# A hybrid decoder layer on one core: means formed with the first job, weights ahead of the quarters, and two groups of loads reordered

## The chip, the cores and the metric

The kernel runs on one core of a Trainium2 chip. The metric is the device time of one execution in microseconds (us); the median of several executions is compared. The engines are TensorE (PE; its weight loads are listed as PEld), VectorE (DVE), ScalarE (ACT), GpSimd (POOL) and SyncE (SP), which issues nearly all DMA transfers from one queue, in order.

## The reference, cut to what matters

One decoder layer over 1,104 tokens (16 meta, 1,024 prompt, 64 sample tokens), width 1,024:

```python
x = x + 0.5 * rmsnorm(swiglu(rmsnorm(x, f1_pre), f1_wg, f1_wu, f1_wd), f1_post)
m, ... = mixer(rmsnorm(x, m_pre), w_in, ..., w_out, ...)   # attention heads + gated short conv
x = x + rmsnorm(m, m_post)
x = x + 0.5 * rmsnorm(swiglu(rmsnorm(x, f2_pre), f2_wg, f2_wu, f2_wd), f2_post)

def rmsnorm(x, g):            # the mean runs over the 1,024 features of a token
    return x * rsqrt(mean(x * x) + eps) * g
def swiglu(x, wg, wu, wd):    # wg, wu: 1024 x 2816, wd: 2816 x 1024
    return (silu(x @ wg) * (x @ wu)) @ wd
```

The mixer projects with `w_in` (24 blocks of 128 columns: q, k, v of four heads, and three conv inputs), runs differential attention over the prompt and over a paged cache for the sample tokens, and projects back with `w_out`. Weights and data are float32.

## The kernel before, in words

**Layout.** Features lie on the 128 partitions, eight chunks `c` of 128 features; tokens lie along the free dimension. The tokens are cut into two halves `p` of 552, each half into two groups `g` of 276. Tile `Y[p]` (`yv`) holds a half's activations, `X[p]` its prepared operands.

**Stages, in order:** gate and up projection 1 (`phase`), down projection 1 (`down`), input projection of the mixer (`phase`), attention, output projection (`down`), gate and up projection 2 (`phase`), down projection 2 (`down`). The places where one hands its result to a `phase` are called hand-overs below: the start of the kernel is the first, down 1 to the input projection the second, the output projection to gate and up 2 the third.

**A norm.** `heads` takes the eight chunks of a half one after the other: ACT squares each (line 221), DVE adds the squares into `ss2` (line 222), ACT multiplies the chunk by the norm's gain in place (line 266). The factor rsqrt(mean) is not applied there: `mean_r` forms it with a matmul against a tile of 1/1024 (line 204) and Ln, Exp and Square on ACT (lines 197 to 199), two DVE operations (200, 201), and stores it in `R[p]`; it is multiplied into the product of a projection, after the matmul. At hand-overs two and three a half's chunks first pass `ready`: the norm of the stage before (lines 543 and 546 on DVE, its own mean kept in `R[p]`), and a store of the chunk to DRAM.

**A job.** A job is a pair of column blocks `u` for a half `p`. Most are done by `seven`: the 2x2 block scheme with seven products instead of eight. A product is four contraction steps, each of three matmuls on high and low parts (`three`, lines 169 to 171). It needs `quarters(p)`: sums of blocks of `Y[p]`, split into high and low part by ACT (line 175) and DVE (line 176), four steps for a half, 7 ACT and 11 DVE operations each; and it needs seven weight pieces, formed likewise from the raw weights in `WR` into `W` (`weights_piece`, lines 326 to 332). While the quarters of the first half and these pieces are not there yet, the first jobs of a phase are `plain`: float32 matmuls (line 296) straight on the gained chunks of `Y`, two per phase, three in the first. `plain` traces a chunk's matmuls and then some steps of the background work (`heads`, then `quarters`). A job's results are read by `Hidden`, `Unit2` and others; for the seven products the first reading is line 420, into the temporaries `n1` (two buffers) and `n5`, which `quarters` uses too.

**Order.** Within an engine the instructions run in the order of a planner, which sorts the traced program by its own estimate of when each is ready, earlier traced work first; a few edges are fixed by hand (`in_turn` for the matmuls, `issue_after`, `keep_in_program_order`). Buffers of one tag are handed on in the order of the program. SP's queue is in order as well: a transfer that waits holds those behind it.

**Weights at a phase's start.** Unit 0 or 1 comes from a copy `early[...]` in DRAM, loaded into `late_raw` (the upper part of `W`); the other is loaded into `WR`.

**Attention and output projection.** `cst` (identity, masks) lies in `WR` from column 1470 on, so the two raw buffers of `load_item` in `down` (`WR` from 0 and from 1024, in turn) partly overlap it.

Of the kernel before, what the change touches and what calls it, by code (L numbers as in the profile page):

```python
# [43 lines left out]
def hybrid_step(ctx: ExitStack, tc: tile.TileContext, ins, outs, n_pool):  # L44
# [104 lines left out]

    last_pe, last_dma = [None], [None]  # L150

# [104 lines left out]

    def heads(p, ready, gain, parts=((0, 1),)):


        ss2 = temp("ss2", HT)  # L260
        for gs in parts:
            t = slice(gs[0] * G, gs[-1] * G + G)
            for n, c in enumerate(ready(gs)):
                x = lay["yv"][p][:, c, :]
                sq_add(ss2, x, n == 0, gs)
                act.activation(x[:, t], x[:, t], AF.Copy, scale=gains[:, gain, c:c + 1])
                yield
            yield
            mean_r(lay["R"][p], ss2, gs)
            yield  # L270

    class Background:
# [15 lines left out]
    def plain(u, p, raw, use, outer, step):  # L288
# [11 lines left out]
        if outer:  # L300
            banks.update({(n, g): bank("mm")[:, :G] for g in range(2) for n in range(2)})
            for n, c in enumerate(PAIR_K):
                in_turn(part, [c], range(2))
                if n:
                    step()
                    if n > 2:
                        step()
            for g in range(2):
                use.plain(g, banks[0, g], banks[1, g])
        else:  # L310
            for g in range(2):
                banks.update({(n, g): bank("mm")[:, :G] for n in range(2)})
                for i in range(0, 8, 2):
                    in_turn(part, PAIR_K[i:i + 2], [g])
                    step()
                use.plain(g, banks[0, g], banks[1, g])

    def weights_of(src):
        dma(wraw, src)

    def weights_piece(n):
# [24 lines left out]
    def phase(n, src, early, late, uses, background, loaded=False, tail=iter(())):  # L346
# [6 lines left out]
        if not loaded:  # L353
            weights_of(src(1 - late))
        dma(late_raw, early)
        for u, p in [(0, 0), (0, 1), (1, 0)][:2 + late]:
            background.need(("h", p))
            if p and not late:
                for m in range(5):
                    weights_piece(m)  # L360
            plain(u, p, raws[u], uses(u, p), p == 0 and u == 0, background.step)
        if late:
            seven([(2, 0), (2, 1), (1, 1)] + [(u, p) for u in range(3, n) for p in range(2)], src, uses, background,
                  tail=tail)
        else:
# [111 lines left out]

    def down(src, blocks, base, order, place, w_src, reuse, g_post, g_pre, res, dst):

# [10 lines left out]
        inputs = [(p, b, i) for p in range(2) for b in range(nb) for i in range(blocks[b])]  # L490
        wt, raws, put = {}, [], []

# [19 lines left out]
        def load_input():  # L512
            p, b, i = inputs.pop(0)
            slot = xs[p][:, base(b) + i]
            dma(f32(slot[:, 0, :]), src(b, i, p))
            put.append(slot)

# [38 lines left out]
        def begin():  # L556
# [5 lines left out]
            yield  # L562
            for n in range(max(blocks[0], 3)):
                if n < 3:
                    split_item()
                    load_item()
                if n < blocks[0]:
# [71 lines left out]
    for c in PAIR_K:  # L639
        dma(lay["yv"][1][:, c, :], ins["x1"][:, c, :])  # L640
    background = Background((("h", 0), heads(0, lambda gs: entering(0), G_F1PRE)),
                            (("h", 1), heads(1, lambda gs: entering(1), G_F1PRE)),
                            (("x", 0), quarters(0)), (("x", 1), quarters(1)))
# [207 lines left out]

    dma(cst, ins["consts"])

# [262 lines left out]
    for step, job in enumerate(jobs):  # L1116
        nxt = step // 9 + 1
        if nxt < H:
# [21 lines left out]
    def place(p, b, q):  # L1140
        if q == 0:
# [3 lines left out]
    begin, run = down(both, (4, 4), lambda b: 4 * b, lambda p, b: (1, 2, 3, 0) if p and not b else (0, 1, 2, 3), place,  # L1145
                      lambda b, q: ins["w_out"][b, q], True, G_MPOST, G_F2PRE, x_spill, x_mid)
    for _ in begin:
# [94 lines left out]
```

## Time and profile before

| | |
|---|---|
| median of 3 runs | 2297.01 us (2293.79 to 2299.85) |
| profiled execution | 2293.83 us, span 2292.1 us |
| PE busy | 2136.1 us, 93% of the span |
| DVE busy | 1404.7 us, 61% |
| ACT busy | 929.5 us, 41% |
| POOL busy | 299.8 us, 13% |
| mean granted TensorE clock | 0.960 |

The span is the profiled stretch from the first to the last instruction of one execution. Busy shares are means over all stages; the stages around the change have shares of their own. The granted clock is 1.00 at 2.4 GHz and 0.50 at 1.2 GHz.

### The profile page before, as it was taken

To read this page: it belongs to the slowest core of one execution; us is meant where nothing else is said; L and a number is where in the kernel's file an instruction comes from. 1 tells how busy PE (TensorE), PEld (TensorE's weight loads), DVE (VectorE), ACT (ScalarE), POOL (GpSimd) and SP (SyncE) were. 2 spreads that over 40 slices of the span, in tenths; PEclk is the share of its full clock that TensorE was granted. 3 is DMA by queue.
4 is the path that set the end of the run, shared out by engine and by line. 5 is a ranking of instruction groups with operands and counts; after the bars stand their busy time and mean duration, and the time that the engine had idled before them with its cause. 6 is when DMAs were issued, how large, how long until landed. Compare 5 with 4: busy or idle time off the path is not lost.

```text
span 2292.1 us, 41517 instructions
## 1 busy us (share of the span) xinstructions
PE 2136.1 (93%) x16126; PEld 2038.4 (89%) x16126; DVE 1404.7 (61%) x2973; ACT 929.5 (41%) x1960; POOL 299.8 (13%) x419
## 2 busy tenths in 40 slices
PE   6899999999999979999799978749999999999997
PEld 5799999999999959999667768739999999999997
DVE  5766556655567775466457656765665665645756
ACT  7433333334254442333235555553333333332522
POOL 0111111110000004443302110001111111100000
PEclk9899999999999989999789889879999999999998
DMA  7121222235444313321567332112122222543443
GB/s 276 55 81 67 81 81 68 81 116 197 130 144 142 131 51 120 124 86 60 191 206 274 125 137 102 67 35 78 67 81 81 68 80 81 175 144 127 141 148 98
DMA packets 115240, 263.48 MB, mean 115 GB/s; under 512 B 14514, under 2 KB 56114, under 8 KB 107602
## 3 DMA queue, kind: packets, MB, share of 16 engines
q1 hardware_dynamic: 109698, 244.92, 31.7%
q0 software_dynamic: 5344, 15.90, 1.9%
q8 instruction: 126, 2.06, 0.4%
q14 instruction: 72, 0.59, 0.1%
HBM read 206.47 MB, written 61.97 MB: 117 GB/s over the span
## 4 chain that ended last, share of the span: by engine, by line
PE 51%; issue 31%; DVE 7%; POOL 5%; DMA 3%; ACT 2%; SPq 1%; POOLq 0%; ACTq 0%; DVEq 0%
PE mm L169 13%; PE mm L170 13%; PE mm L171 13%; POOL u L440 3%; POOL n L440 3%; PE po L982 2%; PE mm L296 2%; PE qk L929 2%; DVE X L176 2%; PE fl L967 1%; PE sa L1059 1%; PE st L204 1%; PE sa L1024 1%; DVE Y L546 1%; DVE Y L543 1%
## 5 line engine op out<-in xcount | busy, mean ns | idle before, releaser
L169 PE MATMUL mm<-X,W 128*128 128x276 f32 x3868 | 1130.1, 292 | 27.8 <-ACT W L175 10.5
L170 PE MATMUL mm<-X,W 128*128 128x276 f32 x3868 | 1127.2, 291 | 2.8 <-DVE X L176 2.8
L171 PE MATMUL mm<-X,W 128*128 128x276 f32 x3868 | 1126.6, 291 | 1.9 <-DVE W L176 1.9
L169 PEld LDWEIGHTS mm<-X,W 128*128 128x128 f32 x3868 | 732.0, 189 | 31.0 <-ACT W L175 11.4
L170 PEld LDWEIGHTS mm<-X,W 128*128 128x128 f32 x3868 | 733.0, 190 | 4.3 <-DVE X L176 4.0
L171 PEld LDWEIGHTS mm<-X,W 128*128 128x128 f32 x3868 | 733.3, 190 | 3.2 <-DVE W L176 3.2
L176 DVE TENSOR_TENSOR W<-WR,W 128x512 fp32r<-128x512 f32 (+3 forms) x421 | 329.1, 793 | 116.4 <-ACT W L175 114.8
L175 ACT ACTIVATE W<-WR 128x512 fp32r<-128x512 f32 (+3 forms) x421 | 284.1, 689 | 249.6 <-PE mm L170 134.8
L420 ACT ACTIVATE n<-mm 128x276 f32<-128x276 f32 x210 | 84.2, 401 | 317.5 <-PE mm L171 299.0
L586 DVE TENSOR_TENSOR Y<-Y,mm 128x276 f32<-128x276 f32 x288 | 126.3, 439 | 128.1 <-PE mm L171 123.4
L440 POOL TENSOR_TENSOR u<-u,R 128x276 f32<-128x276 f32 x93 | 75.1, 807 | 493.2 <-ACT u L471 265.3
L440 POOL TENSOR_TENSOR n<-n,R 128x276 f32<-128x276 f32 x83 | 65.4, 787 | 547.2 <-ACT n L449 547.2
L170 PE MATMUL mm<-X 128*128 128x276 f32 x416 | 121.9, 293 | 2.7 <-DVE X L176 2.7
L169 PE MATMUL mm<-X 128*128 128x276 f32 x416 | 123.0, 296 | 1.5 <-ACT X L175 1.5
L423 DVE TENSOR_TENSOR n<-mm,n 128x276 f32<-128x276 f32 x105 | 46.8, 445 | 125.7 <-PE mm L171 113.9
L171 PE MATMUL mm<-X 128*128 128x276 f32 x416 | 121.4, 292 | 0.0
L221 ACT ACTIVATE sq<-Y 128x276 f32<-128x276 f32 x168 | 68.2, 428 | 86.4 <-DVE Y L586 58.7
L176 DVE TENSOR_TENSOR X<-X 128x552 fp32r<-128x552 f32 x104 | 75.5, 728 | 38.4 <-ACT X L175 37.9
L169 PE MATMUL mm<-X,X 128*128 128x276 f32 x320 | 93.9, 293 | 0.0
L170 PE MATMUL mm<-X,X 128*128 128x276 f32 x320 | 93.1, 291 | 0.0
L171 PE MATMUL mm<-X,X 128*128 128x276 f32 x320 | 93.1, 291 | 0.0
L929 PE MATMUL qk<-q,q 64*128 64x336 f32 (+10 forms) x360 | 69.9, 385 | 15.5 <-ACT q L175 11.1
(174 smaller groups left out, 2669.3 us busy)
## 6 DMA issues: line engine op xcount, KB each, us to landing
WR<-in_w_gu SPq DMA_DIRECT2D x43, 1024.0 KB, 4.8
WR<-in_w_dn SPq DMA_DIRECT2D x48, 640.0 KB, 3.9
X<-hid SPq DMA_DIRECT2D x88, 276.0 KB, 4.1
kp<-in_cache_k SPq DMA_DIRECT2D x64, 256.0 KB, 3.9
vp<-in_cache_v SPq DMA_DIRECT2D x64, 256.0 KB, 4.4
hid<-u SPq DMA_DIRECT2D x93, 138.0 KB, 1.8
hid<-n SPq DMA_DIRECT2D x83, 138.0 KB, 1.7
WR<-in_w_in SPq DMA_DIRECT2D x11, 1024.0 KB, 4.9
```

Of the source, the lines that this page charges most:

```text
L169: nc.tensor.matmul(ps, lh, rh, start=first, stop=False, **kw)
L170: nc.tensor.matmul(ps, lh, rl, start=False, stop=False, **kw)
L171: last_pe[0] = nc.tensor.matmul(ps, ll, rh, start=False, stop=last, **kw).ins
L175: tc.keep_in_program_order(act.activation(hi, raw, AF.Copy))
L176: on.tensor_tensor(lo, raw, f32(hi), op=ALU.subtract)
L221: act.activation(sq, src[:, s], AF.Square)
L296: last_pe[0] = nc.tensor.matmul(banks[n, g], w, lay["yv"][p][:, c, g * G:g * G + G], start=c == PAIR_K[0], stop=c == PAIR_K[-1]).ins
L420: act.activation(t, ps, AF.Copy)
L423: dve.tensor_tensor(self.n1, ps, self.n1, op=ALU.add)
L440: on.tensor_tensor(t, t, lay["R"][p][:, g * G:g * G + G], op=ALU.mult)
L586: dve.tensor_tensor(y, y, ps, op=ALU.add)
L929: last_pe[0] = nc.tensor.matmul(pw[m], a[r, q0:q0 + P], b[r, k0:k1], start=n == 0, stop=n == 2, tile_position=(m * DH, 0)).ins
```

## The change

1. The mean of `heads` is no longer traced at the end of its chunks. A new function `rms` traces it where the factor is first read: in `plain` behind the matmuls of a half's first job (for the second half, behind each group of it), and for the first half of a `down` stage behind tile 7 of the last block. The sums of squares wait in `ss2`, at the kernel's start in `R[p]` itself (`at_r`).
2. In `phase` the weight pieces 0 to 4 are traced ahead of the last plain job in every phase (in the first phase: unit 2 is loaded into `WR` there, and its pieces are no longer left to `seven`). `upto` limits how far the background steps go within each plain job: `heads` of the second half in the first, the first half's quarters in the second, and so on.
3. The load of the early weights into `late_raw` is issued behind the load of the others (`issue_after(last_load[0])`).
4. In the last block of `down`, second half, the steps of `ready` begin one tile later (n > 8), with two at the last tile.
5. Attention: `cst` is a tile of its own and is loaded behind q, k and v. The first piece of `w_out` is loaded at step 4 of the 36 attention steps and split at step 12; `down` is told so (`have`), takes it off its list and splits its four inputs first.

```diff
+    def rms(p, gs):
+        if p in sums_of:
+            mean_r(lay["R"][p], sums_of[p], gs)
+            if gs[-1]:
+                del sums_of[p]
...
-        ss2 = temp("ss2", HT)
+        ss2 = sums_of[p] = lay["R"][p] if at_r else temp("ss2", HT)
...
-            yield
-            mean_r(lay["R"][p], ss2, gs)
-            yield
...
+        def upto(self, name):
+            return lambda: self.step() if any(n == name for n, _ in self.named) else None
...
+            rms(p, (0, 1))
             for g in range(2):
                 use.plain(g, banks[0, g], banks[1, g])
...
+                rms(p, (g,))
                 use.plain(g, banks[0, g], banks[1, g])
...
-        dma(late_raw, early)
-        for u, p in [(0, 0), (0, 1), (1, 0)][:2 + late]:
+        with tc.issue_after(last_load[0]):
+            dma(late_raw, early)
+        jobs = [(0, 0), (0, 1), (1, 0)][:2 + late]
+        for u, p in jobs:
             background.need(("h", p))
-            if p and not late:
+            if (u, p) == jobs[-1]:
+                if late:
+                    weights_of(src(2))
                 for m in range(5):
                     weights_piece(m)
-            plain(u, p, raws[u], uses(u, p), p == 0 and u == 0, background.step)
+            last = ("x", 1) if (u, p) == jobs[-1] else ("x", 0) if p else ("h", 1)
+            plain(u, p, raws[u], uses(u, p), p == 0 and u == 0, background.upto(last))
...
-                        if n % 4 == 3 if nb > 2 else n % 2 if b else n < 10:
+                        if n % 4 == 3 if nb > 2 else n % 2 if b else n < 8:
                             first.step()
-                        if p and b == nb - 1 and g:
+                        if p and b == nb - 1 and n > 8:
                             second.step()
+                            if n == 15:
+                                second.step()
                         if p and b == nb - 1 and n == 7:
+                            rms(0, (0, 1))
                             second = Background(*junction(1))
...
+    cst, = ring("cst", 1, K_W)
...
-    cst = WR[:, 1470:]
...
-    dma(cst, ins["consts"])
...
     load_v(0)
+    dma(cst, ins["consts"])
...
+        if step == 4:
+            dma(WR[:, :1024], ins["w_out"][0, 0])
+        if step == 12:
+            w = W[:, 1024:2048], W[:, 0:1024]
+            halves(w[0], w[1], WR[:, :1024], dve)
+            first_w = {(0, 0, 0): (w[1], w[0])}
```

## Rows read from the trace of the kernel before

**Rows 1.** The page: span, PE's busy time, DVE's group of weight splits.

```profile
span 2292.1 us, 41517 instructions
...
PE 2136.1 (93%) x16126; PEld 2038.4 (89%) x16126; DVE 1404.7 (61%) x2973; ACT 929.5 (41%) x1960; POOL 299.8 (13%) x419
...
L176 DVE TENSOR_TENSOR W<-WR,W 128x512 fp32r<-128x512 f32 (+3 forms) x421 | 329.1, 793 | 116.4 <-ACT W L175 114.8
```

**Rows 2.** PE's waits, whole span: total us, times, longest us.

```profile
PE st L204 <- DVE ss L222: 77.0, 6, 24.0
PE qk L929 <- ACT q L175: 11.1, 1, 11.1
PE mm L169 <- ACT W L175: 10.5, 3, 7.7
```

**Rows 3.** Timeline, first hand-over: start us, duration us, instruction [idle before <-releaser].

```profile
17.90 1.28 ACT L191 ACT_TABLE_LOAD   x1
...
31.92 0.76 ACT L266 ACTIVATE Y<-Y,gains 128x552 f32<-128x552 f32 x1
...
78.72 0.40 ACT L420 ACTIVATE n<-mm 128x276 f32<-128x276 f32 x1 [1.94 <-DVE X L176]
...
80.36 0.60 PE L169 MATMUL mm<-X,W 128*128 128x276 f32 x1 [1.69 <-ACT W L175]
```

**Rows 4.** Stretches: busy us and count by engine, granted clock, DMA share, GB/s.

```profile
36.00:79.00 43.00, 34.59 (x146) 27.92 (x144) 40.27 (x104) 25.20 (x70) 6.65 (x6) 0.91 0.20 69
...
821.00:841.00 20.00, 8.82 (x31) 6.71 (x30) 13.41 (x34) 9.10 (x22) 2.36 (x4) 0.70 0.24 86
841.00:865.00 24.00, 17.79 (x84) 14.73 (x82) 22.88 (x57) 13.31 (x36) 2.17 (x4) 0.93 0.08 27
865.00:870.00 5.00, 4.96 (x22) 4.96 (x23) 0.51 (x1) 0.68 (x2) 0.00 (x0) 0.51 0.61 210
...
1439.00:1483.00 44.00, 40.29 (x273) 39.24 (x274) 30.06 (x81) 23.78 (x62) 0.00 (x0) 0.87 0.20 65
1483.00:1541.00 58.00, 27.50 (x101) 21.30 (x100) 43.64 (x108) 35.40 (x79) 1.54 (x2) 0.74 0.11 39
```

**Rows 5.** Timeline of DVE and PE, second hand-over.

```profile
811.05 0.44 DVE L222 TENSOR_TENSOR R<-R,sq 128x276 f32<-128x276 f32 x1
...
821.53 0.51 DVE L543 SCALAR_TENSOR_TENSOR Y<-Y,gains,R 128x276 f32<-128x276 f32 x1
...
837.20 0.45 DVE L222 TENSOR_TENSOR ss<-ss,sq 128x276 f32<-128x276 f32 x1 [0.68 <-ACT sq L221]
...
865.04 0.60 PE L169 MATMUL mm<-X,W 128*128 128x276 f32 x1 [6.25 <-ACT n L420]
```

**Rows 6.** Timeline of SP, ACT and DVE, start of the attention.

```profile
1106.22 0.33 SPq L153 DMA_DIRECT2D W<-early_w  x1
...
1115.00 2.22 ACT L175 ACTIVATE q<-q 128x1040 fp32r<-128x1040 f32 x2 [14.51 <-DMA q<-q_spill]
...
1121.16 0.50 DVE L939 CUSTOM_DVE_ANT_0 p<-qk,WR 128x336 f32<-128x336 f32 x1
```

**Rows 7.** Timeline of SP, PE and ACT, start of the output projection.

```profile
1344.26 6.05 SPq L153 DMA_DIRECT2D WR<-in_w_out  x2
...
1355.01 0.60 PE L169 MATMUL mm<-X,W 128*128 128x276 f32 x1 [8.60 <-ACT X L175]
...
1365.95 0.40 ACT L584 ACTIVATE Y<-mm 128x276 f32<-128x276 f32 x1 [1.58 <-PE mm L171]
1367.46 0.40 ACT L584 ACTIVATE Y<-mm 128x276 f32<-128x276 f32 x1 [1.11 <-PE mm L171]
```

**Rows 8.** Timeline of PE, third hand-over.

```profile
1439.04 2.21 PE L204 MATMUL st<-ss,onesD 128*128 128x276 f32 x4 [12.72 <-DVE ss L222]
...
1530.80 1.29 PE L204 MATMUL st<-ss,onesD 128*128 128x276 f32 x2 [24.00 <-DVE ss L222]
...
1548.35 0.50 PE L169 MATMUL mm<-X,W 128*128 128x276 f32 x1
```

More of the change, by code (lines that the diff above doesn't have):

```diff
@@ L147, in hybrid_step @@
     c_spill = [dram.tile([P, T], F32, name=f"c_spill{k}") for k in range(4)]
-    last_pe, last_dma = [None], [None]
+    last_pe, last_dma, last_load = [None], [None], [None]
     def dma(dst, src):
@@ L255, in quarters, with heads @@
             yield
-    def heads(p, ready, gain, parts=((0, 1),)):
-        ss2 = temp("ss2", HT)
+    sums_of = {}
+    def rms(p, gs):
[3 more added lines that the diff above has]
+                del sums_of[p]
+    def heads(p, ready, gain, parts=((0, 1),), at_r=False):
+        ss2 = sums_of[p] = lay["R"][p] if at_r else temp("ss2", HT)
         for gs in parts:
@@ L319, in weights_of @@
         dma(wraw, src)
+        last_load[0] = last_dma[0]
     def weights_piece(n):
@@ L354, in phase @@
             weights_of(src(1 - late))
-        dma(late_raw, early)
-        for u, p in [(0, 0), (0, 1), (1, 0)][:2 + late]:
+        with tc.issue_after(last_load[0]):
+            dma(late_raw, early)
+        jobs = [(0, 0), (0, 1), (1, 0)][:2 + late]
+        for u, p in jobs:
             background.need(("h", p))
-            if p and not late:
+            if (u, p) == jobs[-1]:
+                if late:
+                    weights_of(src(2))
                 for m in range(5):
                     weights_piece(m)
-            plain(u, p, raws[u], uses(u, p), p == 0 and u == 0, background.step)
+            last = ("x", 1) if (u, p) == jobs[-1] else ("x", 0) if p else ("h", 1)
+            plain(u, p, raws[u], uses(u, p), p == 0 and u == 0, background.upto(last))
         if late:
-            seven([(2, 0), (2, 1), (1, 1)] + [(u, p) for u in range(3, n) for p in range(2)], src, uses, background,
-                  tail=tail)
+            seven([(2, 0), (2, 1), (1, 1)] + [(u, p) for u in range(3, n) for p in range(2)], src, uses, background, 5,
+                  tail)
         else:
@@ L475, in plain, with down @@
             self.put(t, g)
-    def down(src, blocks, base, order, place, w_src, reuse, g_post, g_pre, res, dst):
+    def down(src, blocks, base, order, place, w_src, reuse, g_post, g_pre, res, dst, have=()):
         X, xs, yv, R = lay["X"], lay["xs"], lay["yv"], lay["R"]
@@ L490, in down @@
         inputs = [(p, b, i) for p in range(2) for b in range(nb) for i in range(blocks[b])]
-        wt, raws, put = {}, [], []
+        wt, raws, put = dict(have), [], []
+        loads = [n for n in loads if n not in wt]
         def key(p, b, q):
@@ L515, in load_input @@
             dma(f32(slot[:, 0, :]), src(b, i, p))
+            last_load[0] = last_dma[0]
             put.append(slot)
@@ L562, in begin @@
             yield
-            for n in range(max(blocks[0], 3)):
-                if n < 3:
+            if have:
+                for n in range(blocks[0]):
+                    split_input()
+            for n in range(3):
+                if n or not have:
                     split_item()
                     load_item()
-                if n < blocks[0]:
+                if not have:
                     split_input()
@@ L640, in hybrid_step @@
         dma(lay["yv"][1][:, c, :], ins["x1"][:, c, :])
-    background = Background((("h", 0), heads(0, lambda gs: entering(0), G_F1PRE)),
-                            (("h", 1), heads(1, lambda gs: entering(1), G_F1PRE)),
+    background = Background((("h", 0), heads(0, lambda gs: entering(0), G_F1PRE, at_r=True)),
+                            (("h", 1), heads(1, lambda gs: entering(1), G_F1PRE, at_r=True)),
                             (("x", 0), quarters(0)), (("x", 1), quarters(1)))
@@ L1145, in hybrid_step @@
     begin, run = down(both, (4, 4), lambda b: 4 * b, lambda p, b: (1, 2, 3, 0) if p and not b else (0, 1, 2, 3), place,
-                      lambda b, q: ins["w_out"][b, q], True, G_MPOST, G_F2PRE, x_spill, x_mid)
+                      lambda b, q: ins["w_out"][b, q], True, G_MPOST, G_F2PRE, x_spill, x_mid, first_w)
     for _ in begin:
```

## The prediction, made before the changed kernel was run

> **What bounds the kernel now.** The page first: PE is busy for 93% of the span [rows 1]; what can be had is the 156 us in which it is idle, and the stretches in which it runs at the lower clock. PE's waits come next, since they say what ended the idle time: 77.0 us in six waits are matmuls of a mean (line 204) that stand in PE's queue and wait for the last square added by DVE, 11.1 us are the first scores, 10.5 us the first weight piece [rows 2]. The means are not needed by the matmuls behind them, which read chunks that were ready long before; so these waits come from order alone. The timelines of PE, DVE and ACT around each wait and the table by stretch come last. They show what is late next: DVE, with 61% over the span, was busy for 40.27 of 43 us at the first hand-over and 22.88 of 24 at the end of the second [rows 4]. So a hand-over can shrink only to what DVE's work and its chains allow.
>
> Why DVE decides: the first reading of a seven-product job (line 420) waited 1.94 us for a DVE split of the quarters [rows 3], since it takes a temporary that the second half's quarters still hold. PE's third product needs that reading. So in every hand-over the third product comes after the second half's quarters, however early PE is; at the second, PE waited 6.25 us for just this, until 865.04 [rows 5].
>
> **First hand-over.** The mean that held PE's first matmuls goes, and PE starts with the first chunk. What counts is when DVE is done. ACT's chunks of the second half ended at 31.92 + 0.76 = 32.7; a table load of 1.28 us [rows 3] and six small operations of some 0.4 us for the first mean stood between them and go behind: 3.7 us, so 29.0. DVE then has the same 43 us of work (36 to 79 [rows 4]), now with three more weight pieces ahead of the last quarters: four or so operations of 0.79 us [rows 1], 3.2 us. That ends at 75.2. Before, the second product began at 80.36 [rows 3] and took 12 matmuls at 5 us for 22 [rows 4], 2.7 us: third product at 83.1. Gain 7.9 us. After a long wait PE runs at the lower clock: from 865 to 870 it was granted 0.51 and began 22 matmuls [rows 4] where the full clock does 12 in 1.51 us (two successive readings [rows 7]), 40 in 5 us; that is 2.2 us lost for a restart. PE will now wait longer here and pays the whole of it; before, it paid about 0.8 behind the third product. **Term: 6 us.** Lower bound 0: the pieces wait for unit 2, which can be loaded only when the second plain job has read `WR`, and DVE waits in its queue for that. Upper bound 17: if the first job does not wait for the quarters, one job (seven products of 1.51 us) is gained on top. I take 6, since the wait of line 420 stands in the rows.
>
> ACT pays for the new place: means now stand between the Silus of the jobs, and each change between Silu and Ln is a table load. Four more here and one at the third, 1.28 us each [rows 3], 6.4 us; ACT's idle time covers them (17.8 of 43 us and 22.6 of 58 [rows 4]), so I charge nothing. Without that cover the sum falls by 6.4. A rule speaks against this more strongly: the Trainium skill, ScalarE: Activation LUTs, What ACT_TABLE_LOAD costs, puts a switch at 2.66 us, a drain of about 1.38 included; five would be 13.3 us, and uncovered the sum would be 48 instead of 61. This trace shows 1.28 us and no drain.
>
> **Second hand-over.** The second group's sum in `R` was complete at 811.5, but the chunks that need it began at 821.53 [rows 5]: its mean stood behind the mean of `ss2` on PE. Now PE takes it after two chunks of the first job. From there to the first chunk I take 3.5 us (PE's mean and some five operations of 0.45 us [rows 5]): 815.0, 6.5 us earlier. Before, another mean with its Ln, Exp and Square stood between the last chunk (837.20) and the quarters; 3 us by the same operations. The 24 us from 841 to 865 that follow are DVE's own and stay. **Term: 10 us**, restart at the lower clock in both. Lower bound 5: only one of these waits goes. Upper bound 17: DVE also fills the 6.6 us that it was idle from 821 to 841 [rows 4].
>
> **Third hand-over.** The wait of 12.72 us until 1439.04 goes, as do those behind it up to 24.00 us until 1530.80 [rows 8]. PE then runs ahead, and DVE has from 1439 what it did until 1541: 30.06 + 43.64 = 73.7 us [rows 4]. Two passes of eight chunks leave it idle, each by the 6.6 us of the pass just read; readings fill some of the first, so 11 in all: 1523.7. Before, the third product began at 1548.35 [rows 8] plus two products of 1.51: 1551.4, at the full clock; now 2.2 are lost at the restart. **Term: 25 us.** Lower bound 12, the first wait alone; upper bound 36, no idle time left. I lean to the middle, because line 176 to 546 alternate with ACT and a store in each chunk, now as before.
>
> **Attention.** The q load stood behind the early weights' load, issued at 1106.22, and its data were split from 1115.00; the first scores were read at 1121.16 [rows 6]. The early load goes elsewhere, and q's place was last read by the first half's job, one job earlier. Now the masks come later: they can't be asked for before some 1106, and 545 KB of them take some 4 us (half of q's 8.8 in company), with lambda behind: first reading near 1113. **Term: 8 us**, bounds 0 (q still goes last) and 11.1 (the whole wait [rows 2]).
>
> **Output projection.** Of two raw loads at 1344.26 the second held SP for most of 6.05 us, until 1350.3, and the inputs stood behind it; PE started at 1355.01 after 8.60 us [rows 7]. Four tiles were done by 1367.46; at 1.51 each that is worth a start at 1361.4. Now the first piece is there and masks no longer lie on the buffer: start at 1346.4, less 2.2 for the clock. **Term: 13 us.** Lower bound 8: inputs asked for only at 1346.4, plus the 4.7 from SP's release to PE's start. Upper bound 15, no clock loss. The piece's split costs some 1.6 us of ACT and of DVE in the attention (twice 0.79), hidden by their idle time there, else 1.6.
>
> **The rest.** `ready` begins a tile later (1.51 us); at the end of the kernel nothing hides it but the doubled last step. **Term: -1 us** (0 to -2). The number of means, chunks and matmuls is the same. The moved early loads are covered by down-stage work and the attention; if one were late, PE would wait for it alone.
>
> **Sum:** 6 + 10 + 25 + 8 + 13 - 1 = 61 us of 2293.8, the profiled execution (span 2292.1 [rows 1]), gives 2232.8. That execution lies 3.2 below the median of the runs, so I forecast 2297.0 - 61 = 2236. All lower bounds give 23, all upper ones 96.
>
> **Rivals.**
> *DVE takes it.* The three hand-overs give their lower bounds, 0 + 5 + 12, because in-order queues planned by estimate leave DVE waiting at the moved means; with the loads' 20, 37 us: 2260. For it: DVE's near-full stretches [rows 4]. Against it: PE's 12.72 and 24.00 us waits had nothing to do with DVE being full.
> *DVE packs.* The upper bounds of the hand-overs, 17 + 17 + 36, and 20: 90 us, 2207. For it: DVE idle for 28 of 102 us from 1439 to 1541 [rows 4]. Against: the chain through ACT in each chunk.
> *The loads stay where they were.* The planner orders SP by its estimate; q or the inputs still come when PE has ended: 41 + 0 + 8 - 1 = 48, 2249.
> *Slower: SP held within the attention.* The out projection's raw load for `WR` from column 0 must wait for the split at step 12. Put into SP's queue right behind the load of step 4, it holds SP for eight of 36 steps of (1346.4 - 1115.0) / 36 = 6.4 us: 51 us in which no cache page is asked for. If pages are late by all of it and the rest gives its 23, the time is 2297 + 51 - 23 = 2325; it decides once the hold exceeds the gain. Against it: the planner issues what it believes ready.
>
> **How the numbers follow.** Forecast 0.46; DVE takes it 0.20; DVE packs 0.15; loads stay 0.11; SP held 0.04; something that cancels to within 0.3% (7 us, about what this measurement can tell) 0.04. The range goes from 4 under the packed case to 8 over the case in which DVE takes it, 2203 to 2268, and leaves out the last two cases and the tails. Faster 0.93, same 0.03, slower 0.04.
>
> **What would show it.** Right: no wait of line 204 above some 5 us; plain matmuls from about 8 us on; third products near 75, and 10, 25 us earlier at the others, each behind a wait for line 420, with DVE over 90% busy before it; scores read some 8 us after the last projection matmul; the output projection begun without a wait over 3 us. Wrong: DVE idle at weight pieces in the first 75 us, SP's transfers bunched in the attention, or third products that do not wait for line 420.

## The result, and the profile after

| | before | changed |
|---|---|---|
| median | 2295.40 us (4 runs, 2288.08 to 2299.85) | 2272.17 us (4 runs, 2267.73 to 2274.74) |
| profiled execution | 2293.83 us, span 2292.1 | 2267.73 us, span 2266.0 |

The ratio is 0.990, 95% interval 0.9869 to 0.9931: faster, by some 23 us. 61 were forecast; the time lies 36 us over the forecast and 4 over the range.

The page of the changed kernel, to [rows 1]: the same work, with five table loads more on ACT.

```profile
span 2266.0 us, 41518 instructions
...
PE 2127.2 (94%) x16126; PEld 2033.7 (90%) x16126; DVE 1405.0 (62%) x2973; ACT 932.9 (41%) x1965; POOL 295.3 (13%) x419
```

PE's waits in it (total us, times, longest us), to be read against [rows 2]. Line 437 is line 420 of before, 305 is 296, 562 is 543, 606 is 584, 954 is 929, 964 is 939.

```profile
PE mm L169 <- ACT n L437: 44.5, 3, 15.2
PE st L204 <- DVE R L222: 12.9, 3, 6.7
PE mm L305 <- DVE u L487: 12.0, 2, 11.3
PE mm L169 <- ACT X L175: 9.4, 6, 4.7
PE mm L169 <- ACT u L437: 8.4, 4, 6.5
PE st L204 <- DVE sq L200: 7.6, 2, 7.0
PE mm L305 <- DMA WR<-in_w_gu: 7.5, 1, 7.5
```

The 77 us of means that waited for `ss` are gone, and so are the 11.1 us before the first scores. In their place stand 44.5 us of line 437, one wait at each hand-over as forecast, and waits that were not there: line 305 on `u`, line 204 on line 200, and the 7.5 us for the first weights, which lay within the first mean's wait before (PE began at 17.4 us). Line 204 on `R` has grown from 5.7 to 12.9, line 437 on `u` from 2.5 to 8.4.

Where the time went is read by PE's progress: the start of the matmul of the same rank in both traces (each has 16126), changed minus before. This lag is read at the matmuls that start at 110, 773, 900, 1345, 1380 and 1600 us in before, and at the last one; its differences are what each stretch gained (a minus is a loss):

| us gained | hand-over 1 | gate, up and down 1 | hand-over 2 | attention | output proj. start | hand-over 3 | rest |
|---|---|---|---|---|---|---|---|
| forecast | 6 | 0 | 10 | 8 | 13 | 25 | -1 |
| changed | -9.5 | -11.8 | 6.8 | 15.8 | 10.1 | 11.9 | 2.8 |
| changed, profiled again (e5) | -10.2 | -13.2 | 6.5 | 12.5 | 8.6 | 11.7 | 1.2 |

The sums are 26.1 and 17.1 us, against spans shorter by 26.1 and 16.8. Down projection 1 alone, from 700 us in before, lost 10.8 and 10.6. The timelines below are rows picked out of their views.

**First hand-over** (timeline of DVE, PE, ACT and SP, to [rows 3]):

```profile
37.72 0.33 SPq L153 DMA_DIRECT2D hid<-u  x1
43.72 0.45 DVE L487 TENSOR_TENSOR u<-mm,R 128x276 f32<-128x276 f32 x1 [6.03 <-DMA hid<-u]
60.38 1.28 ACT L191 ACT_TABLE_LOAD   x1
61.67 0.49 ACT L197 ACTIVATE sq<-st,eps_r 128x276 f32<-128x276 f32 x1
63.11 1.28 ACT L488 ACT_TABLE_LOAD   x1
64.64 9.33 PE L305 MATMUL mm<-Y,W 128*128 128x276 f32 x32 [11.32 <-DVE u L487]
92.03 0.60 PE L169 MATMUL mm<-X,W 128*128 128x276 f32 x1 [14.99 <-ACT n L437]
```

PE starts at 7.5 us instead of 17.4, yet the third product comes at 92.0: forecast 75, before 83.6. DVE stands for 6.03 us because the only buffer `u` is still being stored. The second half's factor is formed at 60 to 63 us, behind the first half's quarters on ACT and DVE; until then the plain job's banks are unread, and PE waits 11.3 us.

**Down projection 1**, timeline of ACT and PE:

```profile
765.39 0.43 ACT L175 ACTIVATE X<-n 128x276 fp32r<-128x276 f32 x1 [2.49 <-DVE n L249]
765.73 0.65 ACT L175 ACTIVATE X<-X 128x552 fp32r<-128x552 f32 x1
766.43 0.60 PE L169 MATMUL mm<-X,W 128*128 128x276 f32 x1 [4.74 <-ACT X L175]
```

An input's split (`X<-X`) stands in ACT's queue behind a quarter's split (`X<-n`) that waits for DVE; PE needs the input. Behind this wait PE runs at the lower clock: it was granted 0.50 from 765 to 770 us.

**Second hand-over** (timeline of PE and DVE, then a stretch; to [rows 5] and [rows 4]):

```profile
831.96 0.74 PE L204 MATMUL st<-R,onesD 128*128 128x276 f32 x2 [4.17 <-DVE R L222]
837.87 0.51 DVE L562 SCALAR_TENSOR_TENSOR Y<-Y,gains,R 128x276 f32<-128x276 f32 x1
854.63 0.45 DVE L222 TENSOR_TENSOR ss<-ss,sq 128x276 f32<-128x276 f32 x1 [0.69 <-ACT sq L221]
879.97 0.60 PE L169 MATMUL mm<-X,W 128*128 128x276 f32 x1 [15.22 <-ACT n L437]
```
```profile
855.00:880.00 25.00, 9.69 (x53) 8.10 (x51) 24.07 (x60) 16.27 (x42) 2.71 (x5) 0.73 0.12 37
```

From the sum to the second group's first chunk it takes 6.0 us (10.0 before), and from the last sum to the third product 24.9 (27.4 before), with DVE busy for 24.07 of 25.

**Attention and output projection** (timeline of SP, PE, DVE and ACT, to [rows 6] and [rows 7]):

```profile
1111.29 0.33 SPq L153 DMA_DIRECT2D q<-q_spill  x1
1123.29 1.51 PE L954 MATMUL qk<-q,q 64*128 64x336 f32 x6 [2.33 <-DVE q L176]
1126.05 0.51 DVE L964 CUSTOM_DVE_ANT_0 p<-qk,cst 128x336 f32<-128x336 f32 x1 [2.82 <-DMA cst<-in_consts]
...
1347.22 0.60 PE L169 MATMUL mm<-X,W 128*128 128x276 f32 x1 [1.82 <-ACT X L175]
1356.04 0.40 ACT L606 ACTIVATE Y<-mm 128x276 f32<-128x276 f32 x1 [1.13 <-PE mm L171]
```

`q` is asked for 9 us ahead of the last projection matmul (its end is near 1120.45), not behind it. The masks are now last, as forecast, and the first scores are read 5.6 us after that matmul; before it was 15.0 (1106.2 to 1121.16 [rows 6]). The output projection waits 1.82 us instead of 8.60.

**Third hand-over** (timeline of PE; then stretches, to [rows 8] and [rows 4]):

```profile
1447.24 1.29 PE L204 MATMUL st<-R,onesD 128*128 128x276 f32 x2 [6.97 <-DVE sq L200]
1469.04 1.29 PE L204 MATMUL st<-R,onesD 128*128 128x276 f32 x2 [6.72 <-DVE R L222]
1516.98 0.60 PE L169 MATMUL mm<-X,W 128*128 128x276 f32 x1 [14.29 <-ACT n L437]
1529.08 0.60 PE L169 MATMUL mm<-X,W 128*128 128x276 f32 x1 [6.52 <-ACT u L437]
```
```profile
1440.00:1462.00 22.00, 15.03 (x93) 13.84 (x91) 21.20 (x60) 14.43 (x40) 0.00 (x0) 0.84 0.05 18
1515.00:1520.00 5.00, 3.02 (x13) 3.02 (x14) 1.78 (x5) 4.69 (x9) 0.00 (x0) 0.50 0.00 0
...
1525.00:1530.00 5.00, 0.92 (x4) 0.92 (x5) 2.33 (x4) 1.61 (x4) 1.28 (x2) 0.55 0.08 28
```

The waits of 12.7 and 24 us became 7.0, 6.7, 14.3 and 6.5. DVE is full while PE waits for the first (21.20 of 22). Behind the third the granted clock is 0.50, behind the fourth 0.55.

### The profile page after: what moved, and what is told of

Its sections match the earlier page's. It is cut to its first block, busy times and chain, and to the rows that moved or that the text cites. A ratio compares the mean times of both kernels' runs of the same rounds, so it can differ in the third digit from the quotient of the medians.

```text
span 2266.0 us, 41518 instructions
## 1 busy us (share of the span) xinstructions
PE 2127.2 (94%) x16126; PEld 2033.7 (90%) x16126; DVE 1405.0 (62%) x2973; ACT 932.9 (41%) x1965; POOL 295.3 (13%) x419
## 4 chain that ended last, share of the span: by engine, by line
PE 37%; issue 14%; DVE 4%; POOL 3%; DMA 2%; ACT 1%; POOLq 0%; DVEq 0%; ACTq 0%; SPq 0%
PE mm L169 10%; PE mm L170 10%; PE mm L171 10%; PE po L1007 2%; PE qk L954 2%; POOL u L457 1%; POOL n L457 1%; PE fl L992 1%; DVE X L176 1%; DMA x_mid<-Y 1%; PE sa L1084 1%; PE sa L1049 1%; DVE Y L562 0%; DVE Y L565 0%; PE po L928 0%
## 5 line engine op out<-in xcount | busy, mean ns | idle before, releaser
L169 PE MATMUL mm<-X,W 128*128 128x276 f32 x3868 | 1132.0, 293 | 61.6 <-ACT n L437 44.5
L305 PE MATMUL mm<-Y,W 128*128 128x276 f32 x320 | 81.7, 417 | 12.0 <-DVE u L487 11.3
```

Of the source, the lines that this page charges most:

```text
L169: nc.tensor.matmul(ps, lh, rh, start=first, stop=False, **kw)
L305: last_pe[0] = nc.tensor.matmul(banks[n, g], w, lay["yv"][p][:, c, g * G:g * G + G], start=c == PAIR_K[0], stop=c == PAIR_K[-1]).ins
```

## The experiments

Each is timed against the kernel before on the same chip; the changed kernel's own ratio was 0.990, and 0.9916 when run again. e1 to e4, e5 to e8, e9 to e12 and e13 to e16 each shared a chip: medians are compared within these groups, ratios across them. All progress is against the one profile of before.

| | median us | ratio | 95% interval | 3rd product, hand-over 1 |
|---|---|---|---|---|
| e1 loads only | 2278.2 | 0.9943 | 0.9928 to 0.9959 | 83.3 |
| e2 quarters later | 2266.2 | 0.9900 | 0.9881 to 0.9918 | 91.8 |
| e3 no limit | 2269.6 | 0.9909 | 0.9892 to 0.9926 | 85.6 |
| e4 second `u` | 2261.2 | 0.9866 | 0.9848 to 0.9885 | 83.6 |
| e5 change again | 2274.0 | 0.9916 | 0.9890 to 0.9941 | 91.7 |
| e6 e2 + e4 | 2254.7 | 0.9844 | 0.9813 to 0.9875 | 83.6 |
| e7 means sooner | 2267.0 | 0.9901 | 0.9873 to 0.9928 | 87.6 |
| e8 e2 + e4 + e7 | 2246.0 | 0.9795 | 0.9768 to 0.9822 | 79.8 |
| e9 own place | 2259.3 | 0.9864 | 0.9840 to 0.9887 | 78.8 |
| e10 e8 + e9 | 2242.1 | 0.9788 | 0.9765 to 0.9811 | 69.5 |
| e11 e8 + POOL adds | 2252.8 | 0.9832 | 0.9805 to 0.9860 | 80.1 |
| e12 e8 + late weights | 2240.8 | 0.9787 | 0.9763 to 0.9811 | 78.7 |
| e13 e10 + late weights | 2245.3 | 0.9814 | 0.9790 to 0.9838 | 78.8 |
| e14 e13, mean at tile 0 | 2247.7 | 0.9823 | 0.9800 to 0.9846 | 78.9 |
| e15 e13, quarters behind | 2241.3 | 0.9781 | 0.9755 to 0.9806 | 79.2 |
| e16 late weights alone | 2267.8 | 0.9901 | 0.9879 to 0.9923 | 89.7 |

**e1.** The kernel before with the hunks of parts 3 and 5 alone.

> The kernel before with parts 3 and 5 of the change alone (early weights behind the others, masks in a tile of their own behind q, k and v, first piece of the output projection's weights loaded and split within the attention). Theory A, that the loads bring nearly all of the change and the three hand-overs with both down projections pay each other off (in the changed kernel PE gains 15.8 us over the attention and 9.3 us at the start of the output projection, 25.1 of 24.7): 2268 to 2274 us, the attention's first scores read within 4 us of the last projection matmul, the output projection's first wait near 2 us. Rival B, that the loads bring what was forecast, 8 + 13, or less, and the hand-overs the rest: 2276 us or above. Rival C, that the attention gains only because PE comes to it later in the changed kernel, and stays with its 11 us wait: near 2284 us.

Rival B: 13 us by the medians, in its range. By PE's progress the attention gains 11.8 and the output projection 8.7, 20.5 where 21 were forecast, and the stages ahead of the attention lose 3.4; rival C is out. So the loads bring at least half of the change, and the rest nets some 10 us, out of gains and losses twice that size.

**e2.**

```diff
+        if p == 0 and not at_r:
+            yield
+            yield
...
-                        if n % 4 == 3 if nb > 2 else n % 2 if b else n < 8:
+                        if n % 4 == 3 if nb > 2 else n % 2 if b else n < 10:
```

> The changed kernel with two steps that do nothing put back at the end of the chunks of a down stage's first half, so that the first half's quarters come as many tiles behind the chunks as before; the mean stays where the change put it. Theory A, that the changed kernel loses 10 us or so between 697 and 773 us because the quarters come eight tiles earlier and hold the input and weight splits behind them in ACT's queue: the lag behind the kernel before is near 10 instead of 20 us after down projection 1, time 2261 to 2266 us. Rival B, that the loss is the mean's new place at tile 7 of the last block or the later start of the second half: no change there, 2270 to 2275 us.

Down projection 1 loses 1.3 us instead of 10.8 (2.8 instead of 11.8 with gate and up 1): theory A by the progress. PE's waits of both kernels, 690 to 800 us, first the changed kernel's, then e2's:

```profile
PE mm L169 <- ACT X L175: 5.8, 3, 4.7
```
```profile
PE mm L169 <- ACT X L175: 0.6, 2, 0.4
```

The ratio hardly shows it: PE reached the attention 6.4 us sooner than in the changed kernel, but left it only 4.2 us sooner and ended 2.8 sooner. e5 and e6 were made to see why.

**e3.** `background.upto(last)` became `background.step if late else background.upto(last)`.

> The changed kernel without the limit on the background steps within the first phase's plain jobs (later phases keep it). Theory A, that the second half's quarters come too late because they may not be traced before the last plain job, while DVE is idle for 12 us in pieces between 37 and 76 us: the third product comes at 80 to 84 instead of 92 us, time 2260 to 2264 us. Rival B, that the weight pieces ahead of the quarters or the means on ACT decide: third product still at 90 to 93 us, 2270 to 2274 us.

Half of A: the third product comes at 85.6, but PE then waits 18.3 us earlier, at 51.25, for a mean behind the quarters (line 200), and 5.3 us are left of the gain in progress; at the end of the profile nothing is (lag -24.3 against -26.1). The ratio can't be told from the changed kernel's. So the limit has a share of the loss here, and without it PE is held by a mean that stands behind the quarters.

**e4.**

```diff
-            t = temp("u")
+            t = temp("ss2", HT)[:, :G] if g and (self.p or at_start[0]) else temp("u")
```

> The changed kernel with a second buffer for the result of a plain job (the place of the sums ss2, which is free there): in the first phase for the second group of each plain job, in the last phase for the second group of the second half. Theory A, that the single buffer u costs 6.03 us of DVE at 37.7 us, which end in the third product at 92 us, and 6.52 us of PE at 1522.6 us: both waits gone, 2259 to 2263 us. Rival B, that at the start the chain of the second half's mean decides and takes the 6 us back (PE still begins its second job's second group near 64 us): only the wait at 1522.6 goes, 2265 to 2267 us. Rival C, that the reading at 1522.6 us then waits for DVE's work of the second group's mean: no change, 2270 to 2274 us.

`at_start[0]` is true in the first phase only. Timeline of PE in e4:

```profile
56.70 9.39 PE L305 MATMUL mm<-Y,W 128*128 128x276 f32 x32 [3.80 <-DVE u L487]
83.57 0.60 PE L169 MATMUL mm<-X,W 128*128 128x276 f32 x1 [14.41 <-ACT n L437]
...
1525.44 0.60 PE L169 MATMUL mm<-X,W 128*128 128x276 f32 x1 [3.25 <-ACT W L175]
```

At the start rival B is wrong: the 11.3 us wait falls to 3.8 and the loss of the first hand-over from 9.5 to 1.3 us. At the third, theory A holds only in part: the wait of 6.52 falls to 1.57, but one of 3.25 us for a weight piece follows, and the hand-over gains 13.6 against 11.9.

**e5, e6.** The changed kernel unaltered, and e2 with e4.

> The changed kernel itself, on the chip of the three runs beside it, so that they have their own measure. Theory: as at first, 0.99 of the kernel before (0.987 to 0.993); of that run's own parts the profile repeats the third product near 92 us, the lag of some 20 us at 773 us and the 6.5 us wait near 1523 us, while the wait of the first cache pages in the attention, 2.8 us in the changed kernel and 7.5 to 7.9 in three runs since, may come out at either. Rival: the page wait follows the kernel and is again 2.8.

> The changed kernel with the second result buffer and with the first half's quarters put back by two steps, each tried alone before. Theory A, that both losses are separate: the lag behind the kernel before is 3 to 5 us after down projection 1 (20.8 in the changed kernel, 12 with either), and the time is 7 to 8 us below that of the second buffer alone, 2253 to 2256 us. Rival B, that what is gained ahead of the attention is lost within it, since the time of the attention is set by the cache pages there and not by when PE comes (the second edit alone came to the attention 7 us sooner and was 0.0% faster): 2259 to 2263 us.

e5 repeats hand-over 1, down 1 and the wait of line 437 on `u`. But the attention of the very same program gained 12.5 us where it had gained 15.8, and in e4, where PE's order in the attention is the same, 11.1. So a difference of 3 to 5 us that arises within the attention of one profile proves nothing, and the 2.2 us that e2 lost there are no more. The wait for the first cache pages came out at 3.6 us, near the 2.8 of the first time: the rival. In e6 theory A holds: 2254.7 beside 2274.0 on the same chip, and a lag of 4.7 us after down projection 1.

**e7.**

```diff
+                    if i == (0 if at_start[0] else 4):
+                        rms(p, (g,))
                     step()
-                rms(p, (g,))
```

> The changed kernel with the second half's means traced ahead of the background steps instead of behind the matmuls: in the first phase behind the first pair of chunks of a group, in the later ones behind the third pair. Theory A, that a factor formed late keeps the plain job's results unread: at the start PE's wait of 11.3 us until 64.6 goes and the third product comes at 84 to 87 instead of 92 us; at the last hand-over the factor stands ahead of the second half's last quarters on ACT and DVE, the wait of 6.5 us at 1522.6 goes and the third product comes 1 to 3 us later by the means' own work; in all 8 to 12 us faster than the changed kernel. Rival B, that the third product only waits for DVE's quarters and these move back by what the means take: no more than 3 us faster. Rival C, that PE now waits at the mean again, as in the kernel before: a wait of line 204 over 5 us at the second or third hand-over, and no gain or a loss.

PE's 11.3 us wait is gone, though the same table loads are made. Timeline of PE in e7:

```profile
34.09 1.28 PE L204 MATMUL st<-R,onesD 128*128 128x276 f32 x2 [6.63 <-DVE sq L200]
87.64 0.60 PE L169 MATMUL mm<-X,W 128*128 128x276 f32 x1 [18.68 <-ACT n L438]
```

By progress it is 4.4 us better than the changed kernel at the first hand-over and 7.3 at the third (19.2 gained), 12 in all as theory A has it; in time 7 beside e5, a little under its range.

**e8.** e2, e4 and e7 together.

> All three edits together: second result buffer, the first half's quarters two steps later, the second half's means ahead of the background steps. Theory A, that the changed kernel loses by order alone and each loss can be taken back: third product near 80 us, no lag over 3 us behind the kernel before after down projection 1, third product of the last hand-over followed by no wait over 3.5 us; 2246 to 2252 us. Rival B, that DVE's work bounds the hand-overs, so that the third mend adds nothing to the other two: within 3 us of these.

Theory A: 2246.0, 28 us under the changed kernel on the same chip. Gate, up and down 1 lose 4.9 and the third hand-over gains 18.1. In all three hand-overs the third product still waits for the reading (line 441 here) and DVE. Timeline of PE:

```profile
79.76 0.60 PE L169 MATMUL mm<-X,W 128*128 128x276 f32 x1 [10.75 <-ACT n L441]
...
1503.58 0.60 PE L169 MATMUL mm<-X,W 128*128 128x276 f32 x1 [15.41 <-ACT n L441]
```

**e9, e10.** The first readings of a phase's first seven-product job go to the free place of `ss2`; e10 adds this to e8.

```diff
+                if n < 2 and self.spare:
+                    if n == 0:
+                        self.pair = temp("ss2", HT)
+                    t = self.pair[:, n * G:n * G + G]
```

> The changed kernel with the first two readings of each phase's first seven-product job put into the place of the sums ss2, which is free by then, instead of n1 and n5. Theory A, that the third product waits for the second half's quarters because they hold n1: the reading of line 437 comes at once behind the first product (near 75 instead of 91.6 us), PE's waits of 15.0, 15.2 and 14.3 us at the three hand-overs shrink to what the weight pieces and the next readings make of them, and the time falls by 10 us or more, to 2255 to 2263 us. Rival B, that the reading stands in ACT's queue behind the splits of the quarters whatever buffer it takes: the waits stay within 2 us and so does the time, 2268 to 2276 us. Rival C, that PE then goes on, but only to the next thing that the quarters hold (the buffers of u, the weight pieces 5 and 6, the second half's operands): the waits of line 437 go and others of line 169 come, with 3 us or less gained at each.

> The three edits of the last run with the own place for the first readings; the second result buffer is used only by the first phase's first two jobs here, since the place is the same. Theory A (the temporaries hold the third product): third product near 70 instead of 79.8 us, 2230 to 2240 us. Rival B (ACT's order holds it): 2243 to 2252 us. Rival C (the next thing holds it): 2238 to 2246 us.

The prediction's central step, tried by itself: the third product comes at 78.8 instead of 92, the 44.5 us of that line are gone, and the first hand-over loses 0.7 instead of 9.5. So the temporaries hold it, not ACT's order. PE's waits in e9:

```profile
PE mm L169 <- ACT u L444: 19.1, 8, 8.0
PE st L204 <- DVE R L222: 12.2, 3, 6.0
PE mm L305 <- DVE u L494: 12.0, 2, 11.3
PE mm L169 <- DVE u L494: 10.1, 1, 10.1
```

Rival C holds for the second and third: `u` holds PE next, and they gain 9.2 and 14.6 instead of 6.8 and 11.9. e10 puts the third product at 69.5, 8.0 us of progress better than e8 there; its time of 2242.1 lies in C's range, and its ratio can't be told from e8's.

**e11.** `dve.tensor_tensor` of line 565 became `gp.tensor_tensor` unless `g_pre is None`.

> The three edits with the residual's addition at the second and third hand-over (line 565, 24 operations at each, 0.45 us or 0.79 us apiece) done by POOL instead of DVE. Theory A, that DVE's amount of work sets the end of the hand-overs: about 12 us less of DVE at each bring the third product 5 to 10 us sooner at both, 2230 to 2240 us. Rival B, that the chain of a chunk (gain and factor on DVE, addition, square on ACT, sum on DVE) sets it, so that a slower addition in the chain lengthens it (POOL took 0.77 us for 276 columns where DVE took 0.45): third products 3 to 8 us later, 2252 to 2262 us.

Rival B for the second hand-over (1.7 us gained, 6.3 in e8), nothing lost at the third (20.4 beside 18.1). An addition took 778 ns in the median on POOL, all shapes, 447 on DVE. By the ratios (0.9832 beside 0.9795) it is some 8 us slower; by progress 4.6 us of it come from the second hand-over and 4.7 from the attention, where the wait for cache pages is 6.8 us instead of 3.0. So the chain of a chunk bounds the second, and less work on DVE brings the third 2 us.

**e12, e16.** Unit 2's load and pieces 0 to 4 left to `seven` in the first phase, on e8 and on the changed kernel.

> The three edits with the first phase's weight pieces left to the seven-product jobs, as in the kernel before. Theory A, that the pieces ahead of the last quarters cost 3 to 7 us at the first hand-over: third product at 75 to 77 us instead of 79.8, or, if the load of unit 2 then comes behind the third plain job, near 83 with a wait for the first piece as before (7.7 us there); 2243 to 2251 us. Rival B, that part 2 is worth its place: third product 3 us or more later than 79.8, 2249 to 2254 us.

> The changed kernel with only the first phase's weight pieces left to the seven-product jobs, as in the kernel before. Theory A, that the pieces ahead of the second half's quarters are a part of the loss at the first hand-over: third product 2 to 5 us sooner than at 92 us, and 2 to 4 us in time. Rival B, that the loss comes by the buffer u and the late means alone: third product at 91 to 93 us, time within 2 us of the changed kernel. Rival C, that the first piece then comes late (PE waited 7.7 us for it in the kernel before): third product later than 94 us.

Theory A in both by direction: at the first hand-over 3.0 us better by progress than e8, and 2.6 than the changed kernel (3.4 than e5), though PE waits 4 to 7 us for the first piece; e12's third product lies between the two cases of A. Timeline of PE in e16:

```profile
81.19 0.60 PE L169 MATMUL mm<-X,W 128*128 128x276 f32 x1 [7.05 <-ACT W L175]
```

The first product is late and the third is not: it no longer waits for the quarters. In time neither e12 (ratio 0.9787, e8's 0.9795) nor e16 can be told from the kernel it starts from.

**e13, e14, e15.** e13 is e10 with e12's late weights. e14 moves `rms(0, (0, 1))` from `n == 7` to `n == 0`. e15 replaces `n % 2 if b else n < 10` by `b == 0 and n < 10`.

> The mends together: first half's quarters two steps later, second half's means sooner, own place for the first readings, second result buffer for the first phase's first two jobs, and the first phase's weight pieces left to the seven-product jobs. Theory A, that the gains add up (the late weights brought 2.6 us at the first hand-over without the own place; the own place 3.9 us in time): 2234 to 2240 us. Rival B, that the own place and the late weights win the same wait, the one of the third product: 2239 to 2244 us.

> As the run beside it, but the first half's mean is traced at tile 0 instead of tile 7 of a down stage's last block. At the third hand-over PE waits some 7 us at the second half's mean for a bank that DVE's reading of the first half's mean (line 200) has not given back. Theory A, that DVE is behind by its own work there (quarters of the first half between evictions and sums), so that with the bank free PE waits as long for the second half's sum (line 222): 0 to 2 us less. Rival B, that the late mean is the cause: 5 us or more of the 7 are gained, in time too. Rival C, that PE then stands at the first half's mean, as in the kernel before (12.7 us): slower by 3 us or more.

> As the first run of this call, but the first half's quarters are traced behind the output projection's last tiles, not among them (the two other hand-overs are left alone). Theory A, that these quarters on DVE delay the sums of the second half and so PE's two waits of 7 and 6 us at line 204 in the third hand-over: both together fall by 6 us or more and the third product there comes 4 to 8 us sooner, 4 to 8 us in time. Rival B, that the quarters have to be done anyway before the third product and DVE has no room for them later: the waits shrink, the one before the seven-product job grows by as much, within 2 us in time. Rival C, that they then hold the second half's chunks on DVE: slower.

e13: rival B, with a loss on top. With the own place the late weights cost 5.6 us of progress at the first hand-over (lag -4.8, -10.4 in e10): there the early pieces are what PE needs next. PE's means (line 204) between 1395 and 1450 us, first e13, then e14, then e15:

```profile
1410.45 1.09 PE L204 MATMUL st<-ss,onesD 128*128 128x276 f32 x4
1421.50 1.28 PE L204 MATMUL st<-R,onesD 128*128 128x276 f32 x2 [6.88 <-DVE sq L200]
```
```profile
1404.94 2.21 PE L204 MATMUL st<-ss,onesD 128*128 128x276 f32 x4 [5.37 <-DVE ss L222]
1425.40 0.73 PE L204 MATMUL st<-R,onesD 128*128 128x276 f32 x2 [3.61 <-DVE R L222]
```
```profile
1419.11 1.09 PE L204 MATMUL st<-ss,onesD 128*128 128x276 f32 x4
1441.84 1.29 PE L204 MATMUL st<-R,onesD 128*128 128x276 f32 x2 [4.17 <-DVE R L222]
```

e14: rival C by progress; in time the three can't be told apart (e15's four runs alone spread from 2235.5 to 2250.7). The wait only changes its name, 5.37 + 3.61 for 6.88, and the hand-over gains 11.0 instead of 16.3. e15: rival B. The first waits shrink, but 3.5 us for a chunk, 5.9 for a mean, 6.7 and 7.3 for `u` follow, and the hand-over gains 15.0, no more than e13's. The order alone moves these waits about; that DVE's work and its chains bound the third hand-over is argued from this and from e11, where less work on DVE brought it 2.3 us.

## Why the prediction was wrong

The direction and the mechanisms of four places were right; the sum was not. Against the forecast the first hand-over is short by 15.5 us of progress, the third by 13.1, gate, up and down 1 by 11.8, the second by 3.2 and the output projection by 2.9; the attention and the end are 7.8 and 3.8 over it. The likeliest case has the loads right (20.5 of 21 in e1) and the hand-overs wrong, and none of the rivals was it: *DVE takes it* (2260) has the right engine but bounds every hand-over at a gain. The argument against it, that PE's waits of 12.72 and 24.00 us had nothing to do with DVE being full, did not carry over: in the new order PE waits beside a DVE that is busy for 21.20 of 22 us.

**First hand-over: the step that failed.** Term 6 with a lower bound of 0; measured -9.5 (e5: -10.2). Right was that DVE's finish of the second half's quarters sets the third product, through `n1` (e9). Wrong was that "DVE then has the same 43 us of work" from 36 us on. It has the same work, but its queue stands still: 6 us for the store of the single `u` (e4: 8.2 us of progress), and again at the means, which the change traces behind the first half's quarters (e7: 4.4). The third share is the weight pieces ahead of the quarters (e16: 2.6); their cost was put at 3.2, which is about right. These shares come from separate runs and need not add, but with the first two taken back the hand-over gains 2.4 us (e8), and with all three 5.4 (e12), near the 6 of the term. The lower bound failed because it named only the wait for unit 2.

**ACT's cover.** "I charge nothing" for the table loads was wrong in place: ACT was idle enough, but one load (60.38) stands in the chain on which PE waited until 64.64, 1.28 us of its 11.3, and the one at 63.11 in that of the next reading. The Trainium skill's rule (ScalarE: Activation LUTs, What ACT_TABLE_LOAD costs) would make each 2.66 us. The trace shows 1.28 and no drain: the first load begins 0.02 us behind the activation ahead of it, and the next activation 0.01 us behind its end. With the means sooner the same number of loads costs no wait of PE for `u` at line 305 (e7).

**Down projection 1: forgotten.** The change takes the mean and two steps out of `heads`, and what follows them, the first half's quarters, moves up by two steps of four tiles each. The prediction counted the means' own work and not what moves up behind them. Price: 10.8 us; put back, 1.3 (e2).

**Second hand-over.** 10 forecast, 6.8. 4.0 of the 6.5 us ahead of the chunks came: Ln stood behind squares and gains on ACT, so that sum to chunk took 6.0 us instead of 3.5. 2.5 of the 3 came behind them; the chunks took a little over 1 us longer. DVE's own 24 us stayed, as said.

**Third hand-over.** 25 forecast, 11.9. The third product was placed right: 1516.98, or 1528.4 without the 11.4 us of progress already gained, against 1551.6 before, 23.2 us sooner. The step that failed is that PE goes on from there. The second group's mean came behind the quarters, its result held `u`, and PE waited 6.52 us more and restarted twice at the lower clock instead of once: 11 us lost between 1517 and 1537. With e4 and e7 the wait is gone and 18.1 are gained (e8). That no wait of line 204 would exceed 5 us was wrong as well: 7.0 and 6.7 remain; e14 shows that the first is not the mean's place, and in e15, where the first half's quarters come later, both shrink (0.7 and 4.2), and other waits take their place.

**Attention.** Term 8; 9.4 at the first reading, masks last, as said. The stage gained 15.8, and 12.5 in e5; what lies over the 9.4 differs from profile to profile, and that it raises the total is luck.

**Output projection.** Term 13; 8.6 to 10.1. Four tiles were done at 1356.04 against 1367.46, of which 1.3 came from the attention's earlier end; the start waited 1.82 us for the inputs' splits, which stand on ACT behind the attention's last norm. Mis-sized by 3 to 4. SP was not held within the attention: the piece was issued at 1212.5 in 0.34 us.

**Tail.** -1 forecast, 1 to 3 gained; too small to be told.

## What to carry to other kernels

When an edit takes a step out of an in-order stream, list what moves up behind it and which queue it now stands ahead of: here that cost 10.8 us, more than the first hand-over's term. When a result is formed later, follow the buffers that wait unread for it (`u`, the banks, `n1`) before summing an engine's work: an engine with the same work finishes later if its queue stands at a single buffer. Whether an early load or split pays depends on what holds the consumer; the weight pieces ahead cost some 3 us while the temporaries held the third product, and brought 5.6 when they did not. e8, e10, e12 and e15 are about 1% faster than the changed kernel. And an edit in one stage can make the planner reorder another, as the next section shows for the attention.

## What was not expected of the hardware

The attention, the same code in sixteen profiles with the new loads besides the changed kernel's own, gained from 4.7 (e9) to 18.1 us (e14) over the profile of before; the same program gave 15.8 and 12.5. One part is PE's wait for cache pages. It goes with the order in which the planner put PE's matmuls there, which edits in other stages changed: the four programs of one order (e1, e2, e7, e11) waited 6.8 to 7.9 us, the three of the changed kernel's order (itself, e4, e5) 2.8 to 3.7, and two further groups (e8 and e12; e10 and e13 to e15) 2.4 to 4.2. The changed kernel's wait and e1's:

```profile
PE sa L1049 <- DMA kp<-in_cache_k: 2.8, 2, 2.6
```
```profile
PE sa L1031 <- DMA kp<-in_cache_k: 7.9, 2, 7.2
```

The gain of the whole attention does not follow this order (7.8 to 13.6 us in the first four, 11.1 to 15.8 in the next three). What sets the rest is open.

After a wait of 14.3 us PE was granted 0.50 (1515 to 1520). The clock had begun to rise (0.80 from 1520 to 1525) when the wait of 6.5 us came; then it was 0.55 (1525 to 1530) and 0.77 (1530 to 1535) before it was 1.00, so here the second wait was paid once more in clock.
